# Small products padded to the whole array in a two-block float32 network on one core

## The chip, the core and the metric

One core of a Trainium2 chip runs the whole network in one launch. The metric is the device time of that launch in microseconds. TensorE (PE) multiplies, loading its weights with an instruction of its own (PEld); VectorE (DVE), ScalarE (ACT) and GpSimd (POOL) do the elementwise work; SyncE (SP) issues most of the transfers. TensorE writes to PSUM banks that the other engines empty.

## The reference

A sequence of S = 512 tokens of D = 1024 passes two blocks. The first mixes (relative attention of 8 heads of 64 beside a short convolution), then runs a mixture of 32 experts, then a gate. The second has an even layer (mLSTM of 4 heads beside NSA, an attention of 8 heads of 64 with compressed, selected and window branches) and an odd layer (HGRN2, 8 heads of 128). What the change touches:

```python
def first_block(...):
    n = rms_norm(h, g_mix[i])
    z = n @ w_in[i] + b_in[i]
    q, k, v, u, bg, cg, ga, gc = jnp.split(z, SPLITS, axis=-1)
    ya = chunked_rel_attention(q, k, v, g_q[i], g_k[i], rel_bias[i])   # q, k normed per head
...
    h = h + hier_moe(n2, w_group[i], b_group[i], w_router[i], b_router[i], w1[i], w3[i], w2[i])
...
def nsa_branch(...):
    qh = partial_rope(rms_norm_2(heads(q, NSA_HEADS), q_norm), pos) * (d ** -0.5)
    ks_h = partial_rope(rms_norm_2(heads(ks, G), k_norm[1]), pos)
    kw_h = partial_rope(rms_norm_2(heads(kw, G), k_norm[2]), pos)
...
    s_c = jnp.einsum('bgrqd,bgnd->bgrqn', q_blk, k_cmp)      # compressed
    s_s = jnp.einsum('bgrqd,bgqnd->bgrqn', q_blk, ks_g)      # selected
    s_w = jnp.einsum('bgrqd,bgkd->bgrqk', q_blk, kwb)        # window
...
def mlstm_branch(...):   # and hgrn2_layer, in the same form
    h = rms_norm_2(h, head_norm)                             # per head
```

## The kernel before

All is float32. To multiply at the fast rate, the kernel splits an operand into a rounded high part and the rest (`split`: an ACT copy and a DVE subtraction) and adds three products: high x high, high x low, low x high. In `proj_T` (L344), `proj_N` (L420) and `Steps.cols` (L254) these are runs of 8 products each over the 8 slices of D, with 128 rows and 128 columns of weights, moving 512 or 256 columns. Weights come in 1 MB chunks by SP.

**The order.** Most of the code lies under a scheduler, which orders each engine's instructions by costs and dependencies and so mixes the projections of a later step among the small products of attention; it may also pull a transfer ahead of where it is written. Parts marked `manual_schedule()` keep the written order: the first norm (`start`), the routing and the experts, the mLSTM and the odd layer.

**Scores.** For a head, `stack_q` puts the high part of q (64 channels) in one half of a 128-row tile and its low part in the other; `stack_k` puts the high part of k in both. So the product of L760 gives high x high and low x high in one. The product of L762 adds high x low, with 64 rows: the half `qh` of q's tile and the low part `kl`. The two heads of a pair use opposite halves in the mixing and the same half in NSA. `softmax_pv` does this for blocks of 128 queries with 256, 256, 384 and 512 keys; then DVE takes the maximum (L766), ACT the exponential (L768), DVE scales, PE transposes (L782), DVE or ACT empties (L786), PE multiplies by V.

**Norms per head.** In the mixing and in NSA, ACT squares each projected tile of two heads (L630), and a float32 product with a 16-column weight tile `blk` (L631 in the mixing, L1602 in NSA) adds the squares over the 64 channels into a 16-row bank `st`. After the root and its reciprocal, the 16 rows are split into `rh`, and per tile two 16-row products with the selector `selr` spread a row over the channels (L653, L1667; tile `rb`). `spread` (L477; tile `gb`) does the same from 4 rows in the mLSTM and the odd layer, where `to_rows` makes the rows.

**Routing and experts.** `moe` loads its constants `mc` on ACT's queue (L803). The routing (L833 to L985) makes each token's slot; `experts` gathers tokens by products (L1114), empties them on ACT (L1116) and multiplies by 192 chunks `wraw` of 1 MB (L1066, L1073), loaded by SP (L1026). 16 of the loads are issued early, into 13 buffers of a ring and three others; each later one waits for a buffer. A branch on the token counts (L1270) stands on every engine ahead of the experts' first work.

**NSA's other parts.** The hidden layer of the compression takes its weights in four loads through the tag "r" of three buffers (L1617), the second two for the values (`in_cmp_v_w`). `rh` holds a buffer of this tag. `ev_gates` (L1512) is a projection with 96 columns. The compressed scores (L1707) have weight tiles of 32 to 128 columns.

Of the kernel before, what the change touches and what calls it, by code (L numbers as in the profile page):

```python
# [19 lines left out]
S = 512  # L20
# [36 lines left out]
def host_layout(inp):  # L57
# [18 lines left out]
    o["ev_w_ifg"] = np.ascontiguousarray(gap(evw).reshape(KT, P, 96).transpose(1, 0, 2))  # L76
# [63 lines left out]
    blk = np.zeros((P, 30), np.float32)  # L140
    blk[np.arange(P), 14 + half] = 1.0 / 64
    sel = np.zeros((16, 8, P), np.float32)
    for t in range(8):
        for p in range(P):
            sel[2 * t + p // 64, t, p] = 1.0
# [3 lines left out]
    o["blk64"], o["sel"] = blk, sel  # L149
# [26 lines left out]
    o["econsts"], eoff = _pack([("blk64", blk), ("cos", cs), ("sin", sn * sgn), ("blkd", (pq // 64 == kc // 64) / 64.0),  # L176
# [7 lines left out]
    hsel = np.zeros((4, 4, P), np.float32)  # L184
    hsel[np.arange(4), np.arange(4)] = 1.0
    o["nconsts"], noff = _pack([("head", hc), ("hsel", hsel.reshape(4, 4 * P)), ("upper", np.where(pq > kc, 1e30, 0.0))])
# [3 lines left out]
    o["oconsts"], ooff = _pack([("head", hc), ("hsel", hsel.reshape(4, 4 * P)), ("res64", r(t % 64 != 0)), ("res128", r(t % 128 != 0)),  # L190
# [85 lines left out]
class Build:  # L276
# [187 lines left out]
    def to_rows(self, wk, u, H, tag="rows"):  # L464
# [4 lines left out]
        r = wk.tile([H, 2, S], F32R, name="rows", tag=tag, bufs=1 if tag == "rows" else 2)  # L469
        self.evac_split(r[:, 0], r[:, 1], ps)  # L470
        return r
# [8 lines left out]
    def start(self, W):  # L480

        n, nc = self.new_n(), self.nc
        with self.tc.tile_pool(name="nrm", bufs=1, reuse_waits="tile") as pool, self.tc.manual_schedule():
# [17 lines left out]
            for s in range(2):  # L501
                part(s, 0)
                self.norm_tile(pool, n, 2 + s, g, xs[s])
            for s in range(2):
                part(s, 1)
# [56 lines left out]
    def setup(self, ctx):  # L562
        tc, nc, I = self.tc, self.nc, self.I
        self.const = ctx.enter_context(tc.tile_pool(name="const", bufs=1, reuse_waits="tile"))
        self.hpool = ctx.enter_context(tc.tile_pool(name="hpool", bufs=1, reuse_waits="tile"))
# [7 lines left out]
        self.mhalf = self.const.tile([P, 1], F32, name="mhalf")  # L573
        nc.vector.memset(self.mhalf, -0.5)
# [10 lines left out]
    def mixing(self):  # L585
        tc, nc, I = self.tc, self.nc, self.I
        V, A, G = nc.vector, nc.scalar, nc.gpsimd
        with ExitStack() as ctx:
# [3 lines left out]
            n, first = self.start(I["w_in"])  # L592
# [4 lines left out]
            at = at_ctx.enter_context(tc.tile_pool(name="a_at", bufs=1, reuse_waits="tile"))  # L597

# [18 lines left out]
            st = psum.tile([16, S], F32, name="st", tag="sc", bufs=3)  # L617
# [4 lines left out]
            selr = at.tile([16, 8, P], F32R, name="selr")  # L622
            for ps, ct in T_tiles(0, 1024):
                z = zz[:, ct]
                ins = A.activation(z, ps, AF.Identity, bias=self.col("b_in", ct))
                if ct == 0:
                    with tc.issue_after(ins.ins):
                        self.copy_act(selr, sel)
                sq = at.tile([P, S], F32, name="sq", tag="sq", bufs=2)
                A.activation(sq, ps, AF.Square, bias=self.col("b_in", ct))  # L630
# [10 lines left out]
            rs = at.tile([16, S], F32, name="rs", tag="sq", bufs=2)  # L641
            A.activation(rs, st, AF.Sqrt, bias=self.epsc[:16])
            V.reciprocal(rs, rs)
            rh = at.tile([16, 2, S], F32R, name="rh")
            self.split(rh[:, 0], rh[:, 1], rs)
# [3 lines left out]
            for t in range(4):  # L649
                for j, g in ((t, gq8), (4 + t, self.col("g_k"))):  # L650
                    rb = psum.tile([P, S], F32, name="rb", tag="tp", bufs=2)
                    for x in range(2):
                        nc.tensor.matmul(rb, selr[:, j], rh[:, x], start=x == 0, stop=x == 1)  # L653
                    V.scalar_tensor_tensor(zz[:, j], zz[:, j], g, rb, op0=OP.mult, op1=OP.mult)
                kl = at.tile([P, S], F32R, name="kl", tag="kl", bufs=1)
                heads = []
                for hh in range(2):
# [3 lines left out]
                    q, qh = self.stack_q(at.tile([P, S], F32R, name="qs", tag="qs%d" % hh, bufs=1), zz[:, t], hh, hh)  # L661
                    k = self.stack_k(at.tile([P, S], F32R, name="ks", tag="ks%d" % hh, bufs=1), zz[:, 4 + t], hh, kl)
                    heads.append((q, qh, k, kl[64 * hh:64 * hh + 64], Vt[:, :, 128 * t + 64 * hh:128 * t + 64 * hh + 64], bias, 64 * hh, None))
# [61 lines left out]
    def stack_q(self, t, z, hh, d, tmp=None):  # L725


# [7 lines left out]
        return t, t[64 * d:64 * d + 64]  # L735
# [9 lines left out]
    def softmax_pv(self, wk, po, heads, first=True, last=True):  # L745
# [8 lines left out]
        for i in range(NT):  # L754
# [3 lines left out]
            for q, _, k, *_ in heads:  # L758
# [35 lines left out]
    def moe(self):  # L794
        tc, nc, I = self.tc, self.nc, self.I
        with ExitStack() as ctx:
# [5 lines left out]
            mc = keep.tile([P, I["mconsts"].shape[1]], F32, name="mc")  # L802
            nc.scalar.dma_start(mc, I["mconsts"])  # L803
# [697 lines left out]
    def ev_gates(self, n, ifg):  # L1501

        nc = self.nc
        w = [(self.wpool if x else self.rawpool).tile([P, KT, 256], F32R if x else F32, name="w" + t, tag="w" + t, bufs=2)[:, :, :96]
# [41 lines left out]
    def nsa(self, mid, n, ifg, y, both):  # L1546
# [4 lines left out]
        qs = [mid.tile([P, S], F32R, name="qs%d" % h) for h in range(8)]  # L1551
        kh = [[mid.tile([P, S], F32R, name="kh%d%d" % (b, g)) for g in range(2)] for b in range(2)]
        kl = [mid.tile([P, S], F32R, name="kl%d" % b) for b in range(2)]
        vv = mid.tile([P, NT, 256], F32, name="vv")
        vc = mid.tile([P, 2, 2, 2, 64], F32, name="vc")
        kc = [mid.tile([P, 2, P], F32R, name="kc%d" % j) for j in range(2)]
        gt = mid.tile([P, NT, 32], F32, name="gt")
        G.memset(vc, 0.0)
        for t in kc:
            G.tensor_copy(t, vc.rearrange("p a b c d -> p (a b c d)")[:, 0:256].rearrange("p (g n) -> p g n", g=2))  # L1560

        with tc.tile_pool(name="e_early", bufs=1, reuse_waits="tile") as wk:
# [15 lines left out]
            for j, (ps, ct) in enumerate(self.ev_tiles(n, 3)):  # L1578
                x, pos = X[j]
                for g in range(2):  # L1580
                    for par in range(2):
                        o = slice(64 * par, 64 * par + 64)
                        for b in range(2):
                            src = ps[64 * g:64 * g + 64, 16 * b:16 * b + 496].rearrange("p (n l two) -> p two l n", l=8, two=2)[:, par]
                            V.tensor_tensor(x[o, 8 * b:8 * b + 8, g, 0:31], src,
                                            pos[o, g, 8 * b:8 * b + 8].unsqueeze(2).to_broadcast([64, 8, 31]), OP.add)
            gq = wk.tile([P, 1], F32, name="gq")
            V.tensor_scalar(gq, self.col("q_norm"), 0.125, None, op0=OP.mult)

            st = psum.tile([16, S], F32, name="st", tag="sc", bufs=3)  # L1590
            zz = wk.tile([P, 6, S], F32, name="zz")
            bo, _ = self.koff["e_blk64"]
            sel = wk.tile([16, 8, P], F32, name="sel", tag="r", bufs=3)
            A.dma_start(sel, I["sel"])
            selr = wk.tile([16, 6, P], F32R, name="selr")
            G.tensor_copy(selr, sel[:, 0:6])
            for c in (2, 0, 1):
                for ps, ct in self.ev_tiles(n, c):
                    A.activation(zz[:, ct], ps, AF.Identity, bias=self.col("ev_b", ct))
                    sq = wk.tile([P, S], F32, name="sq", tag="sq", bufs=1)  # L1600
                    A.activation(sq, ps, AF.Square, bias=self.col("ev_b", ct))
                    nc.tensor.matmul(st, ec[:, bo + 14 - 2 * ct:bo + 30 - 2 * ct], sq, start=ct == 4, stop=ct == 3)  # L1602
            self.ev_tokens(n, 14, vv)
            rs = wk.tile([16, S], F32, name="rs", tag="sq", bufs=1)
            A.activation(rs, st, AF.Sqrt, bias=self.epsc[:16])
            V.reciprocal(rs, rs)
            rh = wk.tile([16, 2, S], F32R, name="rh", tag="r", bufs=3)
            self.split(rh[:, 0], rh[:, 1], rs)
# [45 lines left out]
            self.split(*(t[:, :, 96:128] for t in kc), kz.rearrange("p (g n) -> p g n", g=2))  # L1654
# [5 lines left out]
            cos, sin = (con(x).unsqueeze(1).to_broadcast([P, 2, S]) for x in ("cos", "sin"))  # L1660
            for j in (4, 0, 2):
                r = wk.tile([P, 2, S], F32, name="r", tag="r", bufs=3)
                G.memset(r, 0.0)
                for x in range(2):
                    rb = psum.tile([P, S], F32, name="rb", tag="tp", bufs=2)
                    for u in range(2):
                        nc.tensor.matmul(rb, selr[:, j + x], rh[:, u], start=u == 0, stop=u == 1)  # L1667
                    V.scalar_tensor_tensor(zz[:, j + x], zz[:, j + x], gq if j < 4 else self.col("k_norm", 1 + x), rb,
                                           op0=OP.mult, op1=OP.mult)
# [5 lines left out]
                for x in range(2):  # L1675
                    for hh in range(2):
                        if j == 4:
                            self.stack_k(kh[x][hh], zz[:, 4 + x], hh, kl[x])
# [17 lines left out]
        with tc.tile_pool(name="e_at", bufs=1, reuse_waits="tile") as wk:  # L1696
            self.PR, self.PT, self.EVAC = 4, 3, ()
            pc = []
            for g in range(2):

                ps = psum.tile([P, S], F32, name="sc", tag="sc", bufs=3)
                gr = slice(64 * g, 64 * g + 64)
# [829 lines left out]
```

## Time and profile before

| | |
|---|---|
| median of 3 runs | 1701.44 us (1700.9 to 1703.94) |
| profiled execution, its own time | 1699.2 us |
| its span, first to last instruction | 1697.4 us |
| mean granted clock of TensorE | 0.990 |
| busy: PE, DVE, ACT, POOL | 97%, 44%, 34%, 11% |
| transfers: mean rate | 175 GB/s |
| transfer of `mc` | 436 KB |

Times in the rows are microseconds from the start of the span. TensorE's products are pipelined and their ends are modelled, so the time from one start to the next says what a product takes of the engine, and its duration says less. "PEclk" is the granted clock as a share of full speed. An engine named with a q (SPq, ACTq) is its queue, which issues transfers and waits for them.

### The profile page before, as it was taken

To read this page: it belongs to the slowest core of one execution; us is meant where nothing else is said; L and a number is where in the kernel's file an instruction comes from. 1 tells how busy PE (TensorE), PEld (TensorE's weight loads), DVE (VectorE), ACT (ScalarE), POOL (GpSimd) and SP (SyncE) were. 2 spreads that over 40 slices of the span, in tenths; PEclk is the share of its full clock that TensorE was granted. 3 is DMA by queue.
4 is the path that set the end of the run, shared out by engine and by line. 5 is a ranking of instruction groups with operands and counts; after the bars stand their busy time and mean duration, and the time that the engine had idled before them with its cause. 6 is when DMAs were issued, how large, how long until landed. Compare 5 with 4: busy or idle time off the path is not lost. (4 is left out here: it accounts for less than half of the span.)

```text
span 1697.4 us, 21994 instructions
## 1 busy us (share of the span) xinstructions
PE 1641.5 (97%) x8940; PEld 1165.1 (69%) x8940; DVE 740.1 (44%) x1433; ACT 578.2 (34%) x1136; POOL 193.3 (11%) x221
## 2 busy tenths in 40 slices
PE   7999999996899999999999999999999999999998
PEld 6776688896544444544445877765577798888888
DVE  4257533345212222222124762585557645445452
ACT  4355423232111111101023532385544434335341
POOL 0000000002000000000003300100024302322230
PEclk9999999998999999999999999999999999999999
DMA  6221222364899999999996233210011223122212
GB/s 217 75 87 44 61 92 87 111 237 164 308 359 409 409 409 409 409 408 409 409 409 231 83 103 123 65 71 26 1 42 67 72 71 109 68 75 75 75 50 77
DMA packets 72704, 297.19 MB, mean 175 GB/s; under 512 B 6672, under 2 KB 9232, under 8 KB 63760
## 3 DMA queue, kind: packets, MB, share of 16 engines
q1 hardware_dynamic: 71664, 293.86, 46.1%
q10 hardware_dynamic: 928, 1.82, 0.3%
q8 instruction: 73, 1.20, 0.3%
q14 instruction: 39, 0.32, 0.1%
HBM read 293.16 MB, written 2.10 MB: 174 GB/s over the span
## 5 line engine op out<-in xcount | busy, mean ns | idle before, releaser
L328 DVE TENSOR_TENSOR wlo<-wraw,whi 128x512 fp32r<-128x512 f32 (+1 forms) x192 | 164.7, 880 | 175.1 <-ACT whi L304 117.1
L1066 PE MATMUL py<-wraw,xg 128*64 128x512 f32 x960 | 212.8, 594 | 0.0
L304 ACT ACTIVATE whi<-wraw 128x512 fp32r<-128x512 f32 (+2 forms) x221 | 156.1, 747 | 146.1 <-PE acc L344 99.4
L1066 PEld LDWEIGHTS py<-wraw,xg 128*64 128x64 f32 x960 | 67.2, 137 | 128.8 <-issue 124.7
L1150 DVE TENSOR_TENSOR h<-h,psc 128x512 f32<-128x512 f32 x64 | 43.6, 687 | 174.8 <-PE psc L1146 174.8
L1073 PE MATMUL acc<-wraw,hT 128*64 128x512 f32 x480 | 109.3, 596 | 2.9 <-DMA wraw<-in_w 2.9
L344 PE MATMUL acc<-nhi,whi 128*128 128x512 f32 (+1 forms) x336 | 84.7, 386 | 1.1 <-ACT whi L304 0.6
L344 PE MATMUL acc<-nhi,wlo 128*128 128x512 f32 (+1 forms) x336 | 84.4, 384 | 0.0
L1116 ACT ACTIVATE xg<-psg 128x512 f32<-128x512 f32 x32 | 19.0, 597 | 184.8 <-PE psg L1114 178.4
L344 PE MATMUL acc<-nlo,whi 128*128 128x512 f32 (+1 forms) x336 | 79.8, 379 | 0.0
L1073 PEld LDWEIGHTS acc<-wraw,hT 128*64 128x64 f32 x480 | 33.0, 137 | 65.4 <-issue 58.2
L344 PEld LDWEIGHTS acc<-nhi,whi 128*128 128x128 f32 x336 | 59.0, 192 | 21.4 <-issue 7.3
L344 PEld LDWEIGHTS acc<-nlo,whi 128*128 128x128 f32 x336 | 59.9, 192 | 12.5 <-issue 0.4
L1146 PE MATMUL psc<-ys,PT 128*128 128x512 f32 x256 | 68.2, 407 | 0.0
L344 PEld LDWEIGHTS acc<-nhi,wlo 128*128 128x128 f32 x336 | 58.9, 192 | 12.5 <-issue 0.9
L1146 PEld LDWEIGHTS psc<-ys,PT 128*128 128x128 f32 x256 | 45.6, 188 | 23.8 <-issue 13.8
L768 ACT ACTIVATE pr<-pr,mx 128x128 f32<-128x128 f32 (+3 forms) x96 | 53.6, 559 | 23.0 <-DVE mx L766 21.2
L1377 POOL TENSOR_TENSOR w<-w,cols 128x512 f32<-128x512 f32 x2 | 2.4, 1228 | 491.2 <-DMA w<-in_w_ple_gate 491.2
L782 PEld LDWEIGHTS pst<-consts,pr 128*128 128x128 f32 x240 | 28.3, 140 | 31.3 <-ACT pT L786 20.4
L344 PE MATMUL acc<-hTh,whi 128*128 128x512 f32 (+1 forms) x176 | 45.7, 389 | 3.2 <-ACT zx L1530 1.9
L1090 ACT ACTIVATE hT<-hp 128x512 f32<-128x512 f32 x16 | 9.6, 600 | 111.1 <-PE hp L1088 111.1
L766 DVE CUSTOM_DVE_ANT_0 pr<-sc,fc 128x128 f32<-128x128 f32 (+3 forms) x64 | 30.0, 489 | 39.9 <-PE sc L762 29.1
(505 smaller groups left out, 3207.8 us busy)
## 6 DMA issues: line engine op xcount, KB each, us to landing
wraw<-in_w SPq DMA_DIRECT2D x192, 1024.0 KB
wraw<-in_w_in SPq DMA_DIRECT2D x20, 1024.0 KB
wraw<-in_ev_w_in SPq DMA_DIRECT2D x17, 1024.0 KB
wraw<-in_od_w_in SPq DMA_DIRECT2D x16, 1024.0 KB
wraw<-in_w_o SPq DMA_DIRECT2D x4, 1024.0 KB
wraw<-in_ev_w_out SPq DMA_DIRECT2D x4, 1024.0 KB
wraw<-in_od_w_out SPq DMA_DIRECT2D x4, 1024.0 KB
wraw<-in_w_ple_gate SPq DMA_DIRECT2D x3, 1024.0 KB
```

What stands on the lines that cost most here:

```text
L304: self.nc.scalar.activation(o, i, AF.Copy)
L328: return lambda: (eng or self.nc.vector).tensor_tensor(lo[:, c], raw[:, c], hi[:, c].bitcast(F32), OP.subtract)
L344: self.nc.tensor.matmul(ps[:, t], w[wi][:, k, c0:c0 + P], x[xi][:, k, t], start=n == 0, stop=n == 3 * kt - 1)
L766: nc.vector.tensor_tensor_reduce(out=pr[:, :n], in0=sc[x][:, :n], in1=bias[:, 384 - P * i:512], scale=-1.0, scalar=3e38, op0=OP.add, op1=O ...
L768: nc.scalar.activation(pr[:, :n], pr[:, :n], AF.Exp, bias=mx, scale=-1.0, accum_out=sm[:, x, i:i + 1])
L782: nc.tensor.transpose(ps[:, i * P:(i + 1) * P], pe[x][i][:, j * P:(j + 1) * P], self.ident)
L1066: nc.tensor.matmul(ACC[j][wn == "w3"][64 * e:64 * e + 64], xg[:, 2 * c + k, o + e], raw[:, e, 512 * k:512 * k + 512], start=c == 0 and k = ...
L1073: nc.tensor.matmul(PY[j][x][64 * e:64 * e + 64], HT[j][:, c, e], raw[:, e, 512 * x:512 * x + 512], start=c == 0, stop=c == 3, skip_group_c ...
L1090: A.activation(hT, hp, AF.Copy)
L1116: A.activation(xg[:, k:k + 2], ps, AF.Copy)
L1146: nc.tensor.matmul(ps, PT[j][:, i * P:(i + 1) * P], YS[j][hl][:, n], start=start and hl == 0, stop=stop and hl == 1)
L1150: V.tensor_tensor(hs, hs, ps, OP.add)
```

## The change

Five edits, all on the same data:

1. The second score product has 128 rows: the low part of k gets a tile of its own for each head (four in NSA), of which the other half is zero.
2. The sums of squares are split into high and low and summed by two products with 128 columns of weights, `sum_squares`; the bank `st` has 128 rows, of which 16 are used.
3. The spreads become one product of 128 rows: one constant tile `rows` holds the high parts from row 0 and the low parts from row 32 on, and `selector` makes a weight tile on POOL that picks both. The loaded constants `blk`, `sel` and `hsel` are gone; `by_head` and `zero` make theirs on POOL.
4. The gates' weights and the compressed scores' weights are widened to 128 columns.
5. `mc` is loaded in the mixing, written behind the first 8 column tiles, into a buffer that stays.

```diff
-    def spread(self, sel, h, rows):
+    def selector(self, pool, n, w=1):
+        t = pool.tile([P, n, P], F32R, name="selr")
+        m = lambda o: self.ident[:, o:o + w * n].rearrange("p (n w) -> p n w", w=w).unsqueeze(3).to_broadcast([P, n, w, P // w])
+        self.nc.gpsimd.tensor_tensor(t.rearrange("p n (w c) -> p n w c", w=w), m(0), m(32), OP.add)
+        return t
+
+    def by_head(self, pool):
+        t = pool.tile([P, 14 + P], F32R, name="blk")
+        self.zero(t)
+        for x in range(2):
+            m = slice(64 * x, 64 * x + 64)
+            self.nc.gpsimd.tensor_scalar(t[m, 14 + x:15 + x], self.ident[m, 0:1], 0.0, 1 / 64, op0=OP.mult, op1=OP.add)
+        return t
+
+    def sum_squares(self, pool, st, blk, ct, ps, bias, start, stop, tag, bufs):
+        sq = pool.tile([P, S], F32, name="sq", tag="sq", bufs=1)
+        self.nc.scalar.activation(sq, ps, AF.Square, bias=bias)
+        hl = pool.tile([P, 2, S], F32R, name="sqr", tag=tag, bufs=bufs)
+        self.split(hl[:, 0], hl[:, 1], sq)
+        for x in range(2):
+            self.nc.tensor.matmul(st, blk[:, 14 - 2 * ct:14 - 2 * ct + P], hl[:, x], start=start and x == 0, stop=stop and x == 1)
...
+    def spread(self, sel, h):
         ps = self.psum.tile([P, S], F32, name="gb", tag="tp", bufs=2)
-        for x in range(2):
-            self.nc.tensor.matmul(ps, sel[:, h], rows[:, x], start=x == 0, stop=x == 1)
+        self.nc.tensor.matmul(ps, sel[:, h], self.rows, start=True, stop=True)
         return ps
...  in mixing
+            def constants():
+                fixed.append(self.by_head(at))
+                fixed.append(self.selector(at, 8, 2))
+                fixed.append([at.tile([P, S], F32R, name="kl%d" % hh) for hh in range(2)])
+                for t in [self.rows] + fixed[2]:
+                    self.zero(t)
...
-            blk = at.tile([P, 30], F32, name="blk")
-            A.dma_start(blk, I["blk64"])
-            sel = at.tile([16, 8, P], F32, name="sel", tag="pT", bufs=2)
-            A.dma_start(sel, I["sel"])
...
-                nc.tensor.matmul(st, blk[:, 14 - 2 * ct:30 - 2 * ct], sq, start=ct == 0, stop=ct == 7)
+                self.sum_squares(at, st, blk, ct, ps, self.col("b_in", ct), ct == 0, ct == 7, "pT", 2)
+            A.dma_start(self.mc, I["mconsts"])
...  in softmax_pv
-            for x, (_, qh, _, kl, *_) in enumerate(heads):
-                nc.tensor.matmul(sc[x][:, :m], qh[:, c], kl[:, :m], start=False, stop=True)
+            for x, (q, _, kl, *_) in enumerate(heads):
+                nc.tensor.matmul(sc[x][:, :m], q[:, c], kl[:, :m], start=False, stop=True)
...  in moe
-            mc = keep.tile([P, I["mconsts"].shape[1]], F32, name="mc")
-            nc.scalar.dma_start(mc, I["mconsts"])
+            mc = self.mc
...  in ev_gates
-                nc.tensor.matmul(ps[:96], w[wi][:, k], n[xi][:, k], start=m == 0, stop=m == 3 * KT - 1)
+                nc.tensor.matmul(ps, w[wi][:, k], n[xi][:, k], start=m == 0, stop=m == 3 * KT - 1)
...  in NSA
-            rh = wk.tile([16, 2, S], F32R, name="rh", tag="r", bufs=3)
-            self.split(rh[:, 0], rh[:, 1], rs)
+            self.split(self.rows[0:16], self.rows[32:48], rs)
...
-                        c, m = slice(96 - 32 * hh, 128), 32 * hh + 32
-                        q, k = (qs[4 * g + hh], kc[0][:, g, c]) if x == 0 else (qs[4 * g + hh][gr], kc[1][gr, g, c])
-                        nc.tensor.matmul(ps[:m], k, q, start=x == 0 and hh == 3, stop=x == 1 and hh == 0, skip_group_check=True)
+                        nc.tensor.matmul(ps, kc[x][:, g, 96 - 32 * hh:224 - 32 * hh], qs[4 * g + hh], start=x == 0 and hh == 3,
+                                         stop=x == 1 and hh == 0)
```

## Rows read from the trace of the kernel before

**Rows 1.** Table of stretches: busy us (instructions) by engine, clock, DMA share, GB/s.

```profile
20.00:80.00 60.00, 59.75 (x296) 44.13 (x295) 18.19 (x18) 22.74 (x31) 1.45 (x4) 1.00 0.29 103
80.00:205.00 125.00, 124.87 (x610) 86.84 (x609) 80.23 (x184) 63.24 (x130) 1.25 (x5) 1.00 0.19 64
435.00:920.00 485.00, 482.11 (x2436) 232.86 (x2437) 117.50 (x236) 66.53 (x114) 3.80 (x4) 1.00 1.00 393
1100.00:1140.00 40.00, 37.48 (x159) 26.66 (x157) 35.71 (x53) 31.36 (x52) 6.06 (x4) 1.00 0.25 82
1140.00:1260.00 120.00, 120.00 (x544) 68.91 (x544) 61.84 (x215) 69.38 (x201) 7.81 (x7) 1.00 0.04 12
```

**Rows 2.** Waits of PE, 1260 to 1400.

```profile
PE gb L477 <- DVE y L1949: 1.1, 1, 1.1
```

**Rows 3.** Timeline of PE, 85 to 88: full products of 256 columns.

```profile
86.10 0.64 PE L420 MATMUL acc<-wlo,nhi 128*128 128x256 f32 x4
86.58 0.64 PE L420 MATMUL acc<-whi,nhi 128*128 128x256 f32 x4
```

**Rows 4.** Timeline of PE, 31 to 37.9: sums of squares and full products.

```profile
31.75 1.03 PE L631 MATMUL st<-sq,blk 128*16 128x512 f32 x2
32.71 0.96 PE L344 MATMUL acc<-nhi,whi 128*128 128x512 f32 x3
...
35.83 2.04 PE L344 MATMUL acc<-nlo,whi 128*128 128x512 f32 x8
37.71 0.40 PE L344 MATMUL acc<-nhi,wlo 128*128 128x512 f32 x1
```

**Rows 5.** One line's instructions, L762: count, durations, first and last start, forms.

```profile
L762 PE MATMUL sc<-kl,qs x96: 275/390/502, 103.4 to 1241.8; 64*128 64x256 f32 x48, 64*128 64x384 f32 x24, 64*128 64x512 f32 x24
```

**Rows 6.** Timeline of PE, 98 to 106: start, us, operation, shapes, count.

```profile
98.19 1.19 PE L653 MATMUL rb<-rh,selr 16*128 16x512 f32 x4
99.31 2.14 PE L344 MATMUL acc<-nhi,whi 128*128 128x512 f32 x8
...
102.46 0.34 PE L760 MATMUL sc<-ks,qs 128*128 128x256 f32 x1
102.64 0.86 PE L344 MATMUL acc<-nlo,whi 128*128 128x512 f32 x3
103.43 0.38 PE L762 MATMUL sc<-kl,qs 64*128 64x256 f32 x1
103.74 0.74 PE L344 MATMUL acc<-nhi,wlo 128*128 128x512 f32 x2
```

**Rows 7.** Timeline of PE, 1150 to 1155: scores of NSA.

```profile
1152.60 0.50 PE L762 MATMUL sc<-kl,qs 64*128 64x512 f32 x1
1153.03 0.50 PE L344 MATMUL acc<-hTl,whi 128*128 128x512 f32 x1
```

**Rows 8.** Timeline of ACT, 400 to 436; in brackets the idle time before and its releaser.

```profile
403.37 0.36 ACTq L803 DMA_DIRECT2D mc<-in_mconsts  x1
...
434.25 1.08 ACT L1116 ACTIVATE xg<-psg 128x512 f32<-128x512 f32 x2 [6.37 <-SPq L1270]
```

**Rows 9.** Timeline of DVE, 403 to 418: a subtraction of a split.

```profile
403.48 0.69 DVE L559 TENSOR_TENSOR hTl<-pst,hTh 128x512 fp32r<-128x512 f32 x1 [1.61 <-ACT hTh L558]
```

**Rows 10.** Timeline of PE, 1257 to 1259: a spread in the mLSTM.

```profile
1257.41 0.73 PE L477 MATMUL gb<-rows,hselr 4*128 4x512 f32 x2
1258.07 0.74 PE L420 MATMUL acc<-whi,hTh 128*128 128x256 f32 x4
```

**Rows 11.** Timeline of PE, 1052 to 1067.

```profile
1060.50 2.00 PE L1618 MATMUL ph<-Xv,w 128*128 128x64 f32 x16 [2.04 <-DMA w<-in_cmp_v_w]
```

**Rows 12.** Waits of SP's queue, 300 to 440: total us, times, longest.

```profile
SPq L1026 <- DMA mc<-in_mconsts: 44.1, 1, 44.1
```

**Rows 13.** Timeline of PE, 430 to 440: the end of the gather.

```profile
432.31 0.64 PE L1114 MATMUL psg<-oh,nlo 128*128 128x256 f32 x4
```

**Rows 14.** Timeline of ACT, 0 to 6.

```profile
1.25 0.39 ACTq L619 DMA_DIRECT2D blk<-in_blk  x1
```

More of the change, by code (lines that the diff above doesn't have):

```diff
@@ L139, in host_layout @@
     half = (np.arange(P) // 64)
[L140 to L145, printed above, removed]
     cparts = [("ident", np.eye(P, dtype=np.float32)),
@@ L468, in to_rows, with start @@
             self.nc.tensor.transpose(ps[:, i * P:(i + 1) * P], u[:, i], self.ident)
[L469 to L473 removed]
+        self.evac_split(self.rows[0:H], self.rows[32:32 + H], ps)
+    def spread(self, sel, h):
         ps = self.psum.tile([P, S], F32, name="gb", tag="tp", bufs=2)
[L476 to L477 removed]
+        self.nc.tensor.matmul(ps, sel[:, h], self.rows, start=True, stop=True)
         return ps
[L480 removed]
+    def start(self, W, then):
         n, nc = self.new_n(), self.nc
@@ L503, in start @@
                 self.norm_tile(pool, n, 2 + s, g, xs[s])
+            then()
             for s in range(2):
@@ L573, in setup @@
         self.mhalf = self.const.tile([P, 1], F32, name="mhalf")
+        self.rows = self.const.tile([P, S], F32R, name="rows")
         nc.vector.memset(self.mhalf, -0.5)
@@ L597, in mixing @@
             at = at_ctx.enter_context(tc.tile_pool(name="a_at", bufs=1, reuse_waits="tile"))
+            fixed = []
+            def constants():
[4 more added lines that the diff above has]
+                    self.zero(t)
+            n, first = self.start(I["w_in"], constants)
+            blk, selr, kl = fixed
             gq8 = keep.tile([P, 1], F32, name="gq8")
@@ L650, in mixing @@
                 for j, g in ((t, gq8), (4 + t, self.col("g_k"))):
[L651 to L655, printed above, removed]
+                    V.scalar_tensor_tensor(zz[:, j], zz[:, j], g, self.spread(selr, j), op0=OP.mult, op1=OP.mult)
                 heads = []
@@ L1586, in nsa @@
                                             pos[o, g, 8 * b:8 * b + 8].unsqueeze(2).to_broadcast([64, 8, 31]), OP.add)
+            G.memset(vc, 0.0)
+            for t in kc:
+                G.tensor_copy(t, vc.rearrange("p a b c d -> p (a b c d)")[:, 0:448].rearrange("p (g n) -> p g n", g=2))
+            for t in kl[0] + kl[1]:
+                self.zero(t)
             gq = wk.tile([P, 1], F32, name="gq")
             V.tensor_scalar(gq, self.col("q_norm"), 0.125, None, op0=OP.mult)
-            st = psum.tile([16, S], F32, name="st", tag="sc", bufs=3)
+            st = psum.tile([P, S], F32, name="st", tag="sc", bufs=3)
             zz = wk.tile([P, 6, S], F32, name="zz")
[L1592 to L1596, printed above, removed]
+            blk = self.by_head(wk)
+            selr = self.selector(wk, 6, 2)
             for c in (2, 0, 1):
@@ L1599, in nsa @@
                     A.activation(zz[:, ct], ps, AF.Identity, bias=self.col("ev_b", ct))
-                    sq = wk.tile([P, S], F32, name="sq", tag="sq", bufs=1)
-                    A.activation(sq, ps, AF.Square, bias=self.col("ev_b", ct))
-                    nc.tensor.matmul(st, ec[:, bo + 14 - 2 * ct:bo + 30 - 2 * ct], sq, start=ct == 4, stop=ct == 3)
+                    self.sum_squares(wk, st, blk, ct, ps, self.col("ev_b", ct), ct == 4, ct == 3, "r", 3)
             self.ev_tokens(n, 14, vv)
             rs = wk.tile([16, S], F32, name="rs", tag="sq", bufs=1)
-            A.activation(rs, st, AF.Sqrt, bias=self.epsc[:16])
+            A.activation(rs, st[:16], AF.Sqrt, bias=self.epsc[:16])
             V.reciprocal(rs, rs)
-            rh = wk.tile([16, 2, S], F32R, name="rh", tag="r", bufs=3)
-            self.split(rh[:, 0], rh[:, 1], rs)
+            self.split(self.rows[0:16], self.rows[32:48], rs)
             w2 = wk.tile([P, P + 64], F32, name="w2")
@@ L1660, in nsa @@
             cos, sin = (con(x).unsqueeze(1).to_broadcast([P, 2, S]) for x in ("cos", "sin"))
+            q = [mid.tile([P, 2, S], F32R, name="qs", tag="qs%d" % t) for t in range(4)]
+            qs = [q[h // 2][:, h % 2] for h in range(8)]
             for j in (4, 0, 2):
@@ L1664, in nsa @@
                 for x in range(2):
[L1665 to L1669, printed above, removed]
+                    V.scalar_tensor_tensor(zz[:, j + x], zz[:, j + x], gq if j < 4 else self.col("k_norm", 1 + x),
+                                           self.spread(selr, j + x), op0=OP.mult, op1=OP.mult)
                 z = zz[:, j:j + 2]
```

110 lines of the change are left out of this document (49 added, 61 removed).

## The prediction, made before the result was known

> **What bounds the kernel now.** I read the table of stretches first, then the timeline of TensorE inside the stretches that the diff touches, then the waits, then the queues around the expert ring.
>
> The table says that TensorE (PE) is the bound almost everywhere the diff works: busy 59.75 of 60 us at 20 to 80, 124.87 of 125 at 80 to 205, and all of 120 at 1140 to 1260, where ACT has 69.38 and DVE 61.84 [rows 1]. The exception is 1100 to 1140, where DVE is busy 35.71 of 40 and PE 37.48. In the expert stage (435 to 920) PE is busy 482.11 of 485 us and the transfers run at share 1.00. So a shorter slot on PE should be a shorter kernel, except there and in chains that wait for DVE at the ends of stages, as the 1.1 us that a spread waited for a product on DVE [rows 2].
>
> But "busy" hides what the change is about. The ends of products are modelled, so a slow product and a fast one both look like work. The honest number is the distance from one start to the next. Full products (128 rows, 128 columns of weights) give the scale: four of 256 columns start at 86.10 and the next at 86.58, so 0.12 us each [rows 3]; eight of 512 columns take 35.83 to 37.71, so 0.235 us each [rows 4].
>
> **The change, part by part.**
>
> *Second score products (96).* There are 48 of 256 columns, 24 of 384 and 24 of 512, all of 64 rows [rows 5]; 32 belong to the mixing, 64 to the NSA part. One of 256 columns starts at 103.43 and the next product at 103.74: 0.31 us for half the rows, against 0.12 for all of them [rows 6]. One of 512 starts at 1152.60, the next at 1153.03: 0.43 against 0.235 [rows 7]. So each costs 0.19 us more than a full one, and I take the same for 384. The product ahead pays too: three full ones of 512 columns take 102.64 to 103.43, 0.79 us where 3 x 0.235 is 0.705, so 0.085 more [rows 6]. Padded to 128 rows with zeros, the product is of the kind of its neighbours. Gain: 96 x 0.19 = 18.2 us for the way out of the small product, 96 x 0.085 = 8.2 for the way in. Where two small products follow each other they share these costs, so I take 25 of 26.4; bounds 18 and 27.
>
> *Sums of squares (14 calls, 8 in the mixing, 6 in the NSA part).* The float32 product with 16 columns of weights shows as two records and takes 31.75 to 32.71: 0.96 us [rows 4]. After, two full ones: 0.47. Gain 0.49 each, 0.57 with a way in of the size seen above: 14 x 0.57 = 8.0 us; bounds 5 and 8. What is added is one ACT copy (two of 128x512 take 1.08 us, so 0.54) and one DVE subtraction (0.69 us) a call [rows 8, 9]. In 20 to 80 that is 8 x 0.54 = 4.3 us on ACT's 22.74 and 8 x 0.69 = 5.5 on DVE's 18.19 of 60 [rows 1]: room enough. It also makes the product ready 1.23 us later; the 24 products (24 x 0.235 = 5.6 us) of the next column tile cover that, if the schedule puts them ahead of it.
>
> *Spreads (30 calls).* Two products of 16 or 4 rows become one of 128. In the mixing two calls take 98.19 to 99.31, 0.56 a call [rows 6]; elsewhere a call takes 1257.41 to 1258.07, 0.66 [rows 10]. With a way in of 0.085 us for each run (0.04 a call where two calls follow each other) and 0.235 after: 8 x 0.37 + 22 x 0.51 = 3.0 + 11.2 = 14.2 us. About 8 of the 22 stand in chains with DVE at the end of a stage, like that of [rows 2], where PE would only wait sooner: I take off 4, and keep 10; bounds 6 and 14. The three 128-row selectors and the zero tiles are made on POOL, which is busy 1.45 of 60 us in 20 to 80 [rows 1].
>
> *Gates (24 products) and compressed scores (16).* Their columns grow to 128. Both run among full ones with all 128 rows, and a wider weight tile saves little of a product of 512 columns: 1 us together; bounds 0 and 2.
>
> *The load of the second compression weights.* PE waits 2.04 us for it at 1060.50 [rows 11], because the old split rows hold one of the three buffers of tag "r" until the spreads are done. They live in a tile of their own now, so the first of these two loads needs no product to finish. I take 1 of these 2 us; bounds 0 and 3.
>
> *Routing constants.* SP's queue of expert loads waited 44.1 us for the completion of the transfer of mc [rows 12], which ACT issued only at 403.37 [rows 8]: the early loads behind this wait come late. Without it each can go as its buffer falls free, and all 16 land sooner, the last by as much as the 44.1 us less what the buffers take of it. What is that worth? The gather's last four products start at 432.31 and, at 0.12 us each, end their slots at about 432.8, and the evacuation behind them starts only at 434.25, released by SP's branch behind the landings [rows 8, 13]. So the experts start about 1.5 us sooner: I take 1.5; bounds 0 and 2. More is not to be had. At 434 the same 16 loads have landed in either kernel, and the 17th needs a buffer that PE frees, so from there on the stage runs as before, only shifted. The price is at the start: the scheduler had pulled the old constants, written behind the first norm, to 1.25 us on ACT's queue [rows 14], so mc will stand there, among the first loads of x and weights. 436 KB less the 79 KB of blk and sel, at the 393 GB/s of [rows 1], is 0.9 us. Bounds 0 and 1.1; I take 0.9.
>
> **Sum.** 25 + 8 + 10 + 1 + 1 + 1.5 - 0.9 = 45.6 us. The profiled execution took 1699.2 us, so 1653.6; it lies 2.2 us under the median of the runs, 1701.44, so the median should be about **1656 us**.
>
> One rule of the Trainium skill speaks against the largest term: "TensorE: Matmul & The Clock Gate", Part 3, says of small products that one with few rows takes as long as one with 128, and that the gain is to lay several on different row groups so that they run together. The pairs of heads in the mixing do lie on different halves of the rows; the trace differs from the rule for the lone product, at 0.31 us against 0.12. By the rule the padding of the scores would gain nothing and would cost the overlap of the pairs.
>
> **Rivals.**
>
> *A. The chains become the bound.* With 18 us off the 120 at 1140 to 1260, ACT is busy 69.38 of 102 and DVE 61.84. Each score goes DVE, ACT, DVE, PE, ACT, PE with three banks for scores, so PE could start to wait for banks. For: ACT's share. Against: not one wait of PE of any size in this stretch now, and projections that fill the gaps. If a third of the 44 us on PE is lost that way, 45.6 - 14.7 = 31 us are left: about 1671.
>
> *B. Padding the scores gains nothing, the pairs lose their overlap.* If heads on opposite halves run together, the second of each of the 16 pairs in the mixing is free now and would cost a full slot, 16 x about 0.16 = 2.6 us. Then 45.6 - 25 - 2.6 = 18 us: 1683. Against: the product at 103.43 stands alone, without its pair, and costs 0.31 us [rows 6]. This is what the rule of the skill just named would make of it.
>
> *C. The slow slot belongs to the place, not to the rows.* A small product always changes the bank and breaks into a run of another group, and that may be what costs. Then only fewer products count: 14 x 0.3 for the sums of squares, 30 x 0.2 for the spreads, about 10 us with the rest: 1690. Against: the full score product at 102.46 breaks in just so, and the next product starts 0.18 us behind it, less than 0.235 [rows 6].
>
> *D. Slower.* The product of the sum of squares stands in PE's queue with everything behind it. It now waits for Square, copy and subtraction. If the schedule leaves it where it was, and weight splits stand ahead of copy and subtraction on ACT and DVE (up to another copy and two subtractions of these sizes), each call stops PE for 1.23 + 0.54 + 1.38 = 3.2 us and the column tiles behind it. 14 calls are 45 us and eat the whole gain; it decides from 45.6 / 14 = 3.3 us a call, and a little above that gives about 1705. Against: PE's 5.6 us of other products between two calls.
>
> **Numbers.** Forecast 0.72, A 0.14, B 0.06, C 0.04, D 0.04, half of it beyond its point. The lower end is all terms at their better bound, 27 + 8 + 14 + 2 + 3 + 2 - 0 = 56 us: 1645; as costs of the way in may be larger where the next product is of yet another kind, I go to 1641. The upper end takes in most of A: 1672. A change of under 0.2% (3.4 us) can't be told from none: faster 0.95, same 0.02, slower 0.03.
>
> **What would show it.** Right: the second scores at 0.12 us (256 columns) and 0.235 (512) from start to start, with 0.235 for the product ahead; a call of the sums at 0.47, a spread at 0.235; the mixing stretch about 15 us shorter, the stretch from 1000 to 1260 about 22; the ring's load 7 ahead of 370 us, and no wait for mc. Wrong: PE waits of many us on DVE or ACT in the softmax (A) or on the split squares (D); the padded score still 0.31 us from the next start (C); a first product on PE more than 1.1 us later than now.

## The result and the profile after

The changed kernel takes 1646.01 us (median of 4 runs, 1645.29 to 1648.37), the kernel before 1701.17 beside it: ratio 0.9675, 95% interval 0.9658 to 0.9691, so 55.2 us less (52.6 to 58.2). Forecast were 45.6 us and 1656; 1646 lies inside the stated range. The profiled execution has a span of 1643.7 us, 53.7 less than before.

PE is still the bound. The stretch from 20 to 80 after (columns as in [rows 1]; it is no longer quite the same work, for later work has moved ahead) shows that the added copies, subtractions and POOL work found room:

```profile
20.00:80.00 60.00, 59.73 (x338) 50.02 (x337) 26.80 (x28) 27.82 (x40) 10.46 (x11) 1.00 0.30 108
```

Between 20 and 80, DVE went from 18.19 to 26.80 us of 60, ACT from 22.74 to 27.82, POOL from 1.45 to 10.46 [rows 1], and PE lost nothing by it.

The timeline of PE after, at the places of [rows 4, 6, 7, 10]:

```profile
31.77 0.63 PE L484 MATMUL st<-sqr,blk 128*128 128x512 f32 x2
32.24 2.03 PE L336 MATMUL acc<-nhi,whi 128*128 128x512 f32 x8
...
92.14 0.63 PE L496 MATMUL gb<-rows,selr 128*128 128x512 f32 x2
92.61 2.00 PE L336 MATMUL acc<-nhi,whi 128*128 128x512 f32 x8
...
97.82 0.28 PE L779 MATMUL sc<-kl,qs 128*128 128x256 f32 x1
97.94 0.40 PE L336 MATMUL acc<-nhi,wlo 128*128 128x512 f32 x1
...
1122.27 0.39 PE L779 MATMUL sc<-kl,qs 128*128 128x512 f32 x1
1122.50 0.63 PE L336 MATMUL acc<-hTh,whi 128*128 128x512 f32 x2
...
1212.01 0.40 PE L496 MATMUL gb<-rows,selr 128*128 128x512 f32 x1
1212.24 0.64 PE L412 MATMUL acc<-whi,hTh 128*128 128x256 f32 x4
```

Start to start, a call of the sums takes 0.47 us where it took 0.96; two spreads 0.47 where they took 1.12, one 0.23 where it took 0.66; a second score product 0.12 (256 columns) and 0.23 (512) where it took 0.31 and 0.43. Each is the number that the prediction gave, but these are the clean places. Over all places, summed from start to start, a call of the sums takes 0.60 us on average (before 0.96), and in all calls but one other products stand between its two; a spread takes 0.29 (before 0.61); a second score product takes 0.15, 0.20 and 0.25 at 256, 384 and 512 columns (before 0.26, 0.37 and 0.42).

Where the 53.7 us of the span came from, by the last start of a line of each stage (from the list of one line's instructions):

| last start of | before | after | gained so far |
|---|---|---|---|
| product with V, mixing | 195.3 | 177.6 | 17.7 |
| router logits | 415.0 | 395.3 | 19.7 |
| experts' last product | 916.8 | 897.5 | 19.3 |
| hidden layer of the compression | 1062.2 | 1034.1 | 28.1 |
| product with V, NSA | 1254.0 | 1210.8 | 43.2 |
| product of the odd layer (lv) | 1627.8 | 1574.6 | 53.2 |

Before, these are the lines:

```profile
L790 PE MATMUL po<-pT,V x64: 272/458/644, 117.7 to 195.3; 128*64 128x512 f32 x16, 128*64 128x384 f32 x16, 128*64 128x256 f32 x16, 128*64 128x128 f32 x16
L862 PE MATMUL lgT<-hTh,wrh x16: 276/282/562, 397.4 to 415.0; 128*36 128x256 f32 x16
L1073 PE MATMUL py<-wraw,hT x32: 592/592/643, 907.8 to 916.8; 128*64 128x512 f32 x32
L1618 PE MATMUL ph<-Xv,w x32: 217/275/323, 1055.8 to 1062.2; 128*128 128x64 f32 x32
L790 PE MATMUL po<-pT,vv x128: 272/458/643, 1156.8 to 1254.0; 128*64 128x512 f32 x32, 128*64 128x384 f32 x32, 128*64 128x256 f32 x32, 128*64 128x128 f32 x32
L2222 PE MATMUL lv<-e x32: 379/379/483, 1453.5 to 1627.8; 128*128 128x256 f32 x32
```

After:

```profile
L807 PE MATMUL po<-pT,V x64: 272/458/643, 108.2 to 177.6; 128*64 128x512 f32 x16, 128*64 128x384 f32 x16, 128*64 128x256 f32 x16, 128*64 128x128 f32 x16
L878 PE MATMUL lgT<-hTh,wrh x16: 276/294/562, 376.4 to 395.3; 128*36 128x256 f32 x16
L1089 PE MATMUL py<-wraw,hT x32: 592/592/643, 888.5 to 897.5; 128*64 128x512 f32 x32
L1629 PE MATMUL ph<-Xv,w x32: 217/275/275, 1030.5 to 1034.1; 128*128 128x64 f32 x32
L807 PE MATMUL po<-pT,vv x128: 272/458/643, 1126.4 to 1210.8; 128*64 128x512 f32 x32, 128*64 128x384 f32 x32, 128*64 128x256 f32 x32, 128*64 128x128 f32 x32
L2232 PE MATMUL lv<-e x32: 379/379/483, 1405.4 to 1574.6; 128*128 128x256 f32 x32
```

The gain falls where the padded products are: mixing, NSA, the spreads of the odd layer (in the last 10 us the faster full products, told of below, have a part). The expert stage gives nothing. Two of the prediction's signs can be read here: forecast were about 15 us in the mixing and 22 from 1000 to 1260; the table has 17.7, and 23.9 from the experts' last product to the end of NSA. Of the waits of PE after (1095 to 1236 and 1260 to 1400; total us, times, longest) these are new or longer: transposes of the softmax (L799) that wait for DVE's scaling, a small product of the compressed branch (L1788), and the spread of [rows 2].

```profile
PE pst L799 <- DVE pr L792: 2.6, 2, 1.9
PE pcol L1788 <- DVE r L1781: 1.1, 1, 1.1
...
PE gb L496 <- DVE y L1960: 1.9, 1, 1.9
```

### The profile page after: what moved, and what is told of

Read it like the earlier page. It is cut to its first block, busy times and chain, and to the rows that moved or that the text cites. A ratio compares the mean times of both kernels' runs of the same rounds, so it can differ in the third digit from the quotient of the medians.

```text
span 1643.7 us, 21982 instructions
## 1 busy us (share of the span) xinstructions
PE 1584.9 (96%) x8910; PEld 1160.9 (71%) x8910; DVE 755.1 (46%) x1448; ACT 581.6 (35%) x1149; POOL 211.8 (13%) x235
## 5 line engine op out<-in xcount | busy, mean ns | idle before, releaser
L320 DVE TENSOR_TENSOR wlo<-wraw,whi 128x512 fp32r<-128x512 f32 (+1 forms) x192 | 169.3, 905 | 128.4 <-ACT whi L296 64.5
L296 ACT ACTIVATE whi<-wraw 128x512 fp32r<-128x512 f32 (+1 forms) x221 | 156.4, 748 | 120.6 <-PE acc L336 75.4
L336 PE MATMUL acc<-nhi,wlo 128*128 128x512 f32 (+1 forms) x336 | 81.1, 376 | 0.0
L1162 PEld LDWEIGHTS psc<-ys,PT 128*128 128x128 f32 x256 | 45.6, 188 | 23.7 <-issue 14.6
L799 PEld LDWEIGHTS pst<-consts,pr 128*128 128x128 f32 x240 | 28.3, 140 | 31.9 <-ACT pT L803 19.4
L579 DVE TENSOR_TENSOR ys<-acc,ys 128x512 fp32r<-128x512 f32 x30 | 20.8, 692 | 59.0 <-ACT ys L578 59.0
L799 PE MATMUL pst<-consts,pr 128*128 128x128 f32 x240 | 45.2, 283 | 2.6 <-DVE pr L792 2.6
```

Source lines behind the costliest of these rows:

```text
L296: self.nc.scalar.activation(o, i, AF.Copy)
L320: return lambda: (eng or self.nc.vector).tensor_tensor(lo[:, c], raw[:, c], hi[:, c].bitcast(F32), OP.subtract)
L336: self.nc.tensor.matmul(ps[:, t], w[wi][:, k, c0:c0 + P], x[xi][:, k, t], start=n == 0, stop=n == 3 * kt - 1)
L579: nc.vector.tensor_tensor(lo, ps, hi.bitcast(F32), OP.subtract)
L799: nc.tensor.transpose(ps[:, i * P:(i + 1) * P], pe[x][i][:, j * P:(j + 1) * P], self.ident)
L1162: nc.tensor.matmul(ps, PT[j][:, i * P:(i + 1) * P], YS[j][hl][:, n], start=start and hl == 0, stop=stop and hl == 1)
```

## The experiments

**One part at a time.** Theory: each small product costs its own slow slot, and the parts add up. Rivals B, C and D deny it for the scores or for the sums.

Scores alone, in the kernel before:

```diff
-            for x, (_, qh, _, kl, *_) in enumerate(heads):
-                nc.tensor.matmul(sc[x][:, :m], qh[:, c], kl[:, :m], start=False, stop=True)
+            for x, (q, _, _, kl, *_) in enumerate(heads):
+                nc.tensor.matmul(sc[x][:, :m], q[:, c], kl[:, :m], start=False, stop=True)
...
+            kl = [at.tile([P, S], F32R, name="kl%d" % hh) for hh in range(2)]
+            for t in kl:
+                self.zero(t)
```

> The kernel before with the second score product alone padded to 128 rows (low part of k in zero-padded tiles of its own, made on POOL). Prediction: 25 us less (18 to 27), so about 1676. Rival B (padding gains nothing, the pairs lose their overlap): 0 to 3 us more. Rival C (the slow slot belongs to the place): no difference, and the product still 0.31 us from the next start at 256 columns.

Measured: ratio 0.9833 (0.9813 to 0.9853) to 1701.93, so 28.4 us less (25.0 to 31.8). The product takes 0.12 us, 103.24 to 103.36:

```profile
103.24 0.28 PE L767 MATMUL sc<-kl,qs 128*128 128x256 f32 x1
103.36 0.63 PE L344 MATMUL acc<-nhi,wlo 128*128 128x512 f32 x2
```

B and C fall: nothing but the rows of the product, and the tile that holds them, was changed, at the same places. What B builds on does exist in the kernel before. Where the second products of a pair of the mixing, on opposite halves, stand side by side, both together take 0.31 us, 129.28 to 129.59:

```profile
129.28 0.39 PE L762 MATMUL sc<-kl,qs 64*128 64x256 f32 x2
129.59 0.39 PE L760 MATMUL sc<-ks,qs 128*128 128x256 f32 x1
```

A pair of the NSA part, on the same half, takes 0.43 (1159.92 to 1160.35). But only three of the 16 pairs of the mixing stand so; every other small product there stands alone and pays for itself.

Forecast were 25, at the edge of the interval. Summed from start to start over all places of the two profiled executions, the second products go from 31.6 to 17.5 us and the products just ahead of them from 24.5 to 14.2, 24.5 us together; the spans differ by 24.3. So the way out, 18.2 in the prediction, gave 14.1, and the way in, 8.2, gave 10.4. That the way in can be dearer than was read shows in a stretch of the kernel before where full and small products of 512 columns alternate:

```profile
109.64 0.49 PE L762 MATMUL sc<-kl,qs 64*128 64x512 f32 x1
110.06 0.50 PE L760 MATMUL sc<-ks,qs 128*128 128x512 f32 x1
110.49 0.50 PE L762 MATMUL sc<-kl,qs 64*128 64x512 f32 x1
110.92 1.90 PE L344 MATMUL acc<-nhi,whi 128*128 128x512 f32 x7
```

The full product at 110.06 holds 0.43 us, as much as the small one: a lone full product between two small ones pays 0.2 us, not the 0.085 read ahead of one small product.

Sums alone:

```diff
-                sq = at.tile([P, S], F32, name="sq", tag="sq", bufs=2)
-                A.activation(sq, ps, AF.Square, bias=self.col("b_in", ct))
-                nc.tensor.matmul(st, blk[:, 14 - 2 * ct:30 - 2 * ct], sq, start=ct == 0, stop=ct == 7)
+                self.sum_squares(at, st, blk, ct, ps, self.col("b_in", ct), ct == 0, ct == 7, "pT", 2)
...  and the same in NSA
```

> The kernel before with the sums of squares alone changed (copy, subtraction, two products of 128 columns). Prediction: 8 us less (5 to 8), so about 1693. Rival D (the product waits for copy and subtraction with everything behind it): no gain, and PE waits of 1 us or more at each of the 14 calls.

Measured: 0.9936 (0.9918 to 0.9954), 10.9 us less (7.8 to 14.0). D falls: the waits of PE in 0 to 100 of this kernel are those of the start and of a weight split, and none for the split squares; in the NSA part (960 to 1100) there is none for them either:

```profile
PE pst L460 <- DVE xs L449: 9.8, 2, 8.7
PE acc L344 <- ACT whi L304: 0.6, 1, 0.6
...
```

This edit changes two things at once, the columns and the type of the product, and no run changes one alone. The trace of the kernel before tells them apart in part. A plain float32 product with 128 rows and 128 columns of weights stands in it too, not split, and shows as two records like the sum's:

```profile
1177.59 1.02 PE L1737 MATMUL po<-pcs,vc 128*128 128x512 f32 x2
1178.44 0.27 PE L782 MATMUL pst<-consts,pr 128*128 128x128 f32 x1
```

It takes 0.85 us; the sum's call with 16 columns takes 0.96 [rows 4]. So most of this gain comes from splitting the operand, and little from the width. Nor is all of the 10.9 us the sums': PE waits 0.98 us for the second compression weights here, not 2.04, and the same 64 products of the hidden layer and 24 of the gates take 13.85 us (1038.68 to 1052.53) where they took 16.49 (1049.76 to 1066.25), 2.6 us less.

Spreads alone:

```diff
     def spread(self, sel, h):
         ps = self.psum.tile([P, S], F32, name="gb", tag="tp", bufs=2)
-        for x in range(2):
-            self.nc.tensor.matmul(ps, sel[:, h], rows[:, x], start=x == 0, stop=x == 1)
+        self.nc.tensor.matmul(ps, sel[:, h], self.rows, start=True, stop=True)
```

> The kernel before with the 30 spreads alone made one product of 128 rows each, with selectors from POOL and the split rows in a tile that stays. Prediction: 10 us less (6 to 14) and up to 3 from the load of the second compression weights, which no longer shares its buffers with the rows: 1688 to 1692. If all 30 calls stood on the path it would be 14.

Measured: 0.9928 (0.9906 to 0.9951), 12.3 us less (8.3 to 16.0). PE no longer waits for the load of the compression weights, in this kernel as in the changed one. The timeline of PE in the changed kernel, at the place of [rows 11]:

```profile
1030.50 1.89 PE L1629 MATMUL ph<-Xv,w 128*128 128x64 f32 x16
1032.20 0.47 PE L1528 MATMUL acc<-hTh,whi 128*128 128x512 f32 x1
1032.51 1.89 PE L1629 MATMUL ph<-Xv,w 128*128 128x64 f32 x16
```

The three together make 51.6 of the 55.2 us.

**The rest: the constants, or where tiles lie.** Comparing the traces of before and after, I found that full products of 512 columns, which nothing in the diff touches, take less: 72 of them run from 1470.16 to 1487.14 before and from 1422.09 to 1438.68 after, 0.236 and 0.230 us each; 96 of 256 columns behind them take 0.120 and 0.114. The chains of work before (first) and after (second):

```profile
1470.16 16.98 PE acc L254 x72
1487.14 11.53 PE acc L420 x96
```

```profile
1422.09 16.59 PE acc L246 x72
1438.68 10.91 PE acc L412 x96
```

The constants' tile is new in the pool ahead of all others, so it moves every tile behind it, the normed input n first of all; the layout leaves the split weights where they were. To tell this from the move of the transfer I ran four kernels: the kernel before and the changed one with an unused tile of 32 bytes ahead, as in this diff, and the kernel before with the constants alone moved, without and with that tile.

```diff
         self.const = ctx.enter_context(tc.tile_pool(name="const", bufs=1, reuse_waits="tile"))
+        self.const.tile([P, 8], F32, name="shift")
```

> The kernel before with one unused tile of 32 bytes a partition ahead of all other tiles: no instruction changes, the tiles of the normed input only start 32 bytes later. Theory of the address: full products of 512 columns take 0.229 us instead of 0.234 from start to start when the tile they stream starts 32 bytes past a multiple of 64, and those of 256 columns with that tile as weights 0.114 to 0.117 instead of 0.120. About 1400 products of the first kind and 420 of the second move: 9 to 10 us less than before. Rival (full products are faster in the changed kernel because fewer small products stand among them): no difference, within 3 us.

> The changed kernel with the same unused tile of 32 bytes ahead, which takes the normed input back to a multiple of 64. Theory of the address: 9 to 11 us more than the changed kernel's 1646, so 1655 to 1657, and the full products back at 0.234. Rival (fewer small products): 1646, within 3 us.

> The kernel before with the routing constants alone moved to the mixing and to a tile that stays (3488 bytes a partition, so the normed input starts 32 bytes past a multiple of 64). Forecast of the prediction for this edit: 1.5 us gained at the start of the experts, up to 0.9 lost at the start of the kernel. Theory of the address: another 9 to 10 us gained by it, so 10 to 11 us less than before. Rival: 0.6 to 1.5 us less.

> The same with 32 unused bytes more, so that the normed input starts at a multiple of 64 as before. This is the move of the constants by itself: 0.6 to 1.5 us less than before by the prediction, and by both theories.

Measured: 0.9971 (0.9957 to 0.9986) for the shift alone, 4.9 us less; the shift in the changed kernel 0.9693 (0.9671 to 0.9715), 3.1 us over the changed kernel's 0.9675, intervals overlapping; the constants alone 0.9960 (0.9942 to 0.9977), 6.8 us less; the constants with n back at a multiple of 64, 0.9971 (0.9959 to 0.9984), 4.9 less. As stated, the theory fell: the kernel before with its 32 bytes does not get the fast products. But the other two do as it said: the run of 72 takes 16.92 us in the changed kernel with the shift, and 16.59 in the kernel before with the constants. So the place matters, only not within 64 bytes. The layout puts n at bytes 19840 (before), 19872, 23328 (constants), 23360, 25376 (after) and 25408 of a partition; fast are 23328 and 25376, both 32 past a multiple of 256. Four more places in the changed kernel:

> The changed kernel with 64 unused bytes ahead of all tiles; the normed input starts 96 bytes past a multiple of 256. Full products of 512 columns have taken 0.229 us at 32 past (two kernels) and where the streamed tile lies 224 past, and 0.233 to 0.234 at 64, 128 and 160 past. If the place within 256 bytes decides, with a fast part around 0: 0.234 here. If only the exact places seen so far are fast: 0.234 too.

> The same with 128 bytes: 160 past a multiple of 256, where the kernel before with 32 bytes showed 0.2335. If the place within 256 bytes decides: 0.234. If it is the place within 128 (or 64) and something else slowed that kernel: 0.229.

> The same with 192 bytes: 224 past a multiple of 256. If the place within 256 bytes decides: 0.229, and the time that of the changed kernel. If only the exact places seen so far are fast: 0.234 and 3 to 5 us more.

> The same with 224 bytes: a multiple of 256. If a fast part of the 256 bytes lies around 0: 0.229. If a start at an odd multiple of 32 is needed as well: 0.234.

The runs of 72 and of 96 in the chains of the changed kernel shifted by 32, 64, 128, 192 and 224 bytes:

```profile
1425.13 16.92 PE acc L246 x72
1442.05 11.39 PE acc L412 x96
```

```profile
1417.89 16.84 PE acc L246 x72
1434.73 11.39 PE acc L412 x96
```

```profile
1423.62 16.91 PE acc L246 x72
1440.53 11.31 PE acc L412 x96
```

```profile
1424.68 16.47 PE acc L246 x72
1441.15 11.51 PE acc L412 x96
```

```profile
1427.43 16.90 PE acc L246 x72
1444.33 11.36 PE acc L412 x96
```

| n past a multiple of 256 | 0 | 32 | 64 | 96 | 128 | 160 | 224 |
|---|---|---|---|---|---|---|---|
| us each, 512 columns, n streamed | 0.235 | 0.230 | 0.235 | 0.234 | 0.236 | 0.235 | 0.229 |
| us each, 256 columns, n as weights | 0.118 | 0.114 | 0.119 | 0.119 | 0.120 | 0.118 | 0.120 |

In all ten layouts the pace goes with the place within 256 bytes, and differently for a streamed tile and for weights. Places 32, 64 and 160 were seen in two kernels each, which agree; since each two also agree within 512 bytes, a period of 512 is not ruled out. Why 32 and 224 and not 0, no run here shows. What it is worth as time is less sure. The times of the last four do not follow the products: 1642.38 us at a shift of 64 bytes (slow products), 1648.41 at 192 (the fastest of 512 columns), 1648.76 at 128 and 1653.66 at 224. But each is one run, and the 29 runs of the kernel before beside the first four spread from 1697.05 to 1707.92, so single times can't settle it. That a layout moves other things too is shown by the shift in the kernel before: its 4.9 us (2.4 to 7.3) are mostly not its products (16.98 to 16.90).

**The transfer of the constants.** The last edit meant to put it back into the expert stage, with the tile where it is:

```diff
-            A.dma_start(self.mc, I["mconsts"])
...  in moe
             mc = self.mc
+            nc.scalar.dma_start(mc, I["mconsts"])
```

> The changed kernel with the transfer of the routing constants back at the start of the expert stage, in the same tile, so that no address moves. Prediction: 0.6 to 1.5 us more than the changed kernel (its early loads gain 1.5 and its place at the start costs up to 0.9). By the run of the constants alone, 5 us under the kernel before: up to 5 us more, which would mean that the start of the experts is worth more than the gap of 1.5 us in front of their first product.

Measured: 0.9673 (0.9656 to 0.9690), the changed kernel's own time. But the edit did not do what I meant. The list for the tile shows the transfer at 1.2 us, as in the changed kernel:

```profile
L819 ACTq DMA_DIRECT2D mc<-in_mconsts x1: 387/387/387, 1.2 to 1.2; - x1
```

The scheduler pulls a transfer ahead when its buffer is free; it is the tile of its own that sets the time, not the line. So this run says nothing of a late transfer. The kernel with the constants alone and n back at a multiple of 64 does, at the start of the experts:

```profile
431.39 0.64 PE L1116 MATMUL psg<-oh,nlo 128*128 128x256 f32 x4
431.95 3.65 PE L1068 MATMUL acc<-wraw,xg 128*64 128x512 f32 x16
```

The experts' first product now starts 0.56 us after the gather's last four; before it was 2.59 us, from 432.31 [rows 13] to 434.90. The changed kernel shows the same, 413.54 and 414.11. In the five traces with late constants this distance is 1.18 to 2.59 us, in the nine with early ones 0.56 or 0.57.

## Why the prediction was right, point by point

**Second scores (forecast 25, measured 28.4; 24.5 summed over the trace).** Right in mechanism and sum. Its two halves were mis-sized against each other, the way out 18.2 for 14.1 and the way in 8.2 for 10.4; that they nearly cancel is luck. The rule of the Trainium skill that was weighed ("TensorE: Matmul & The Clock Gate", the row on small-K matmuls under "Why this matters for your kernels", with Part 3) does not hold for the lone product here: with 64 rows it took 0.31 us, with 128 it takes 0.12. Its other half, that products on different row groups run together, agrees with the pair at 129.28. And in a run of small products the price is paid once: four spreads of 16 rows take 1.12 us [rows 6], four full products of 512 columns 0.94. The Trainium skill, "TensorEngine Tiling (Array Packing)", section "Key Properties", says that a change of tiling mode drains TensorE; the alternating stretch, 0.43 us for every product, agrees.

**Sums of squares (8, measured 10.9).** The interval holds both, in part by luck: 2.6 of the 10.9 us are the load's, and the sums' own products gave 5.3 us (13.5 to 8.2, summed from start to start) where 14 x 0.49 = 6.9 were forecast. The delay by copy and subtraction stayed hidden, as forecast.

**Spreads and the load of the compression weights (10 + 1, measured 12.3 together).** The sum was right. The load was under-sized. The same 64 products of the hidden layer and 24 of the gates took 16.49 us and now take 1025.54 to 1039.27, 13.73 us with four other small products (0.45 us) among them: 3.2 us less for a term of 1, the gates' wider weights included. With the wait of 2.04 us goes what came behind it: in 1062.5 to 1066 of the kernel before the granted clock was 0.51, about the lower of its two levels (1.2 GHz), and nine products took the 3.5 us:

```profile
1062.50:1066.00 3.50, 3.50 (x9) 2.24 (x9) 1.70 (x6) 2.15 (x3) 0.95 (x1) 0.51 0.00 0
```

The same products now run at a granted clock of 1.00. Some of the spreads gained nothing, as was allowed for: the one of [rows 2] waits 1.9 us for DVE instead of 1.1.

**Routing constants (1.5 less 0.9).** Both halves came, and in this execution neither lasted. At the start the first product on the normed input moves from 14.05 to 14.46 us, but the first sum of squares starts at 31.77 where it was 31.75. The experts' first product gains the gap. Then "from there on the stage runs as before, only shifted" holds for most of the stage: the first expert product comes 20.8 us sooner (434.90, now 414.11), and one behind PE's wait for a chunk still 20.6 (857.32, now 836.75). The last one comes only 19.3 sooner. The 1.3 us between go just behind that wait, 2.9 us in both kernels: there the granted clock falls to 0.50, the lower level, where it stayed at 1.00 before (858 to 860):

```profile
837.00:839.50 2.50, 2.50 (x7) 1.40 (x5) 0.00 (x0) 0.00 (x0) 0.00 (x0) 0.50 1.04 411
```

In the kernel with the constants alone nothing is lost: it is 4.8 us ahead at the stage's first product and 4.9 at its last. Why the clock falls behind the same wait in one execution and not in another, no run here shows.

**The sum (45.6, measured 55.2).** The measured interval, 52.6 to 58.2, does not hold the forecast. The runs of the three padded terms add up to 51.6, but the load's part is in two of them, 2.6 us in the run of the sums, so some 49 are theirs. Gates and compressed scores (forecast 1) had no run of their own, and half of the 16 compressed scores had 64 rows, not 128 as the prediction says. What the prediction left out is that a tile ahead of all others moves the rest: the full products became faster by 2% in the mixing and the odd layer, and by the pair with and without the shift that is some 3 us. Since the shift in the kernel before is worth 5 us for other reasons, the split between this and the constants stays open.

**Rivals.** A holds for 4 us, no more: waits of 2.6 and 1.1 us from the compressed branch to the end of the softmax; before, there was none from 1140 to 1260. B, C and D fell, each by the run that changes one part; the overlap that B builds on is there, in three pairs.

## What to carry to other kernels

Read the price of a small product from start to start, and that of its neighbours with it: a full product between two small ones can pay as much as they do. The price lies where small and full products change over, so a lone small product pays most and a run of them pays once. Where PE is the bound and the small product needs little data, padding it with zeros to the rows of its neighbours is the cheap cure; that padding the columns of weights alone helps, no run here shows. Look at the type as well: the sums of squares were slow mostly because they were plain float32. When a tile is added ahead of others, look at products that the change does not touch before crediting the change.

## What the runs showed of the hardware that was not expected

Two products of 64 rows on opposite halves that follow each other take 0.31 us together, on the same half 0.43 (256 columns, kernel before). A plain float32 product of 512 columns takes 0.85 us with 128 columns of weights and 0.96 with 16.

Full products of 512 columns take 0.229 to 0.230 us when the streamed tile lies 32 or 224 bytes past a multiple of 256 in its partition, and 0.234 to 0.236 at 0, 64, 96, 128 and 160; those of 256 columns with that tile as weights take 0.114 at 32 and 0.118 to 0.120 elsewhere.
